# A two-layer trunk (RG-LRU, then forgetting attention): projections one step on, one tile for all pairs' keys and queries, squares behind the tanhs, sums kept in SBUF

## The chip, the cores and the metric

The kernel runs on one core of one Trainium2 chip. Its time is the device time of one execution in microseconds (us); the figure compared is the median over the runs of a kernel. TensorE is PE in the profile (its weight loads are PEld), VectorE is DVE, ScalarE is ACT, GpSimd is POOL, and SP is the engine that issues most of the DMAs and all the DMA transposes.

## The reference

The input is 1024 positions of width 1024 in float32. Two residual layers and a last norm are computed:

```python
h = rms_norm(x, g0)                       # layer 0: RG-LRU
u = h @ w_in                              # two halves of width 1536
xc = causal conv of width 4 over the first half
r, i = sigmoid(block_diag(xc, wa) + ba), sigmoid(block_diag(xc, wx) + bx)   # 12 blocks of 128
a = exp(-8 * r * softplus(-a_param))
hs = scan over positions of  a * previous + sqrt(1 - a*a) * (i * xc)
x = x + (hs * silu(second half)) @ w_out
h = rms_norm(x, g1)                       # layer 1: attention with a forget gate
q, k, v, gate, f = h @ w_in               # 16 heads of 64, f: one logit for each head
cum = cumsum(log_sigmoid(f + b_f))
p = softmax(q k^T / 8 + cum[query] - cum[key], causal)
x = x + ((p v) * silu(gate)) @ w_out
out = rms_norm(x, final_g)
```

## The kernel before

Products in full precision are made from three matmuls: both operands are cut into a high and a low part (names with `h` and `l`: `wh` and `wl` of a weight, `hh` and `hl` of the normed input, `qkh` and `qkl` of keys and queries). ACT makes the high part of a weight (line 90), DVE or POOL the low part (line 101). All matmuls are issued by the helper on line 60, most DMAs by `fetch` and the like on line 57.

**Layer 0** (up to about 430 us) loops over 12 blocks `n` of 128 channels: projections (`ups`, `gps`), convolution, two gates (tanhs on ACT, line 322), scan, and pieces of the output projection as filling work. Beside it the kernel computes the squared norm of each value weight, which later bounds the values: `squares_of_values` loads a piece of `wv` (128x512, 256 KB) into one of the `wf` buffers that the weights also use, and ACT squares and sums it (line 405). There are 16 pieces, two for each block from n = 3 on.

**Layer 1.** A prologue (430 to 560 us) makes the first values, the forget gate and pair 0's keys and queries. Heads come in pairs: head `hd` is half `s = hd % 2` of pair `hd // 2`. A projection of one half of the positions (a unit) is 24 matmuls in four steps of six. Its result goes to the tiles `qkh` and `qkl` (one set for keys, one for queries), and from there DMAs on SP's queue copy rows into the operand tiles: `T0` or `T1` for keys (one for each `s`), and for queries `U` (positions 0 to 511, shared by both `s`) and `U0` or `U1` (positions 512 to 1023).

For each head there are two stretches of work, called runs, written by a table of characters: `.` takes one step of filling work (`fill`) and one of the DMAs that load operands (`side`), a digit takes a step of attention.

- First run: `weigh(hd, 0)` (the product with the values, PSUM tile `O`) and `maxima(hd, 1)` (the logits `S` of the second 512 queries, their maximum on DVE, exp on ACT, weights `pp`, and a DMA transpose `pT<-pp` on SP's queue, line 806).
- Second run: `weigh(hd, 1)` and `maxima(hd + 1, 0)`.

The operand DMAs (`pieces`) stand on the same SP queue between the transposes. In the first run come `U` of hd + 1 and the second half of `T` of hd + 1; in the second run `U0`/`U1` of hd + 1, which `maxima(hd + 1, 1)` reads in the next run, and the first half of `T` of hd + 2. The filling of an even head is the next pair's keys (first half), queries (first half) and keys (second half); that of an odd head its queries (second half) and the gate, two halves. The key and query tiles are taken anew for each pair, in the same memory.

From head 12 on the filling is the output projection. `partial` (16 groups of 36 matmuls) loads 512 positions of the residual (`xp<-x1d`, into one of two `R` buffers), adds the product of six pairs on DVE (line 915) and stores the sum through POOL's queue (line 916). `turned` then loads the sums again (`x<-x1d`), transposes them on PE into a PSUM bank of tag `g`, adds the last two pairs' product, squares on ACT and multiplies by `grow`, the last norm's factors (line 974); only then is the bank free. `grow` is loaded behind head 15's first run into a `sg` buffer.

A scheduler with a time model of its own fixes the order of the instructions on each engine; engines and the SP queue take them strictly in that order. The pools that matter here: PSUM tags `g`, `S` and `O` with two buffers each, `wf` three, `p` two, `pp` four, `R` two.

Of the kernel before, what the change touches and what calls it, by code (L numbers as in the profile page):

```python
# [35 lines left out]
def f32(ap):  # L36
    return ap.bitcast(F32)
# [3 lines left out]
def trunk(ctx: ExitStack, tc: tile.TileContext, xt, w0, wg, wo0, pc, gn, gf, w1, wv, wf, bf, wo1, out):  # L41
# [146 lines left out]
    with ExitStack() as l0:  # L188
# [207 lines left out]

        vsq = const.tile([P, 4, 4], F32, name="vsq")

        def squares_of_values():

            for g, i in itertools.product(range(4), range(4)):
                wt = loaded((2, 256))
                nc.sync.dma_start(wt, wv[g, :, 2 * i : 2 * i + 2])
                flat = wt.rearrange("p a b -> p (a b)")
                nc.scalar.activation(flat, flat, AF.Square, accum_out=vsq[:, g, i : i + 1])
                yield
# [3 lines left out]
        for n in range(NB):  # L410
            wu = first[0] if n == 0 else list(weights(w0[n]))
            if n == 1:
                ups = both = [ps.tile([P, HALF], F32, tag="g", name="ups") for h in range(2)]
            else:
                ups = two_banks("ups")
                both = [ups.rearrange("p a b -> p (a b)")]
                ups = [ups[:, h] for h in range(2)]
            product(ups[0], 0, wu)
            if n == 0:
                gps = held[0] = two_banks("gps")  # L420
                product(gps[:, 0], 0, first[1])
# [62 lines left out]
        def value_bounds():  # L484

            g2 = const.tile([P, KT], F32, name="g2")
            nc.vector.tensor_tensor(g2, gnt[:, 1], gnt[:, 1], ALU.mult)
            g2 = g2.rearrange("p (k two) -> p k two", two=2)
            most = const.tile([P, 4], F32, name="most")
            nc.vector.tensor_tensor(most, g2[:, :, 0], g2[:, :, 1], ALU.max)  # L490
            nc.vector.tensor_tensor(vsq, vsq, most.unsqueeze(1).to_broadcast([P, 4, 4]), ALU.mult)
            all_ = ps.tile([P, 16], F32, tag="O", name="vnorm")
            matmul(all_, onesf, vsq.rearrange("p a b -> p (a b)"), start=True, stop=True)
            nc.vector.tensor_reduce(
                scale_v, all_.rearrange("p (a b) -> p a b", b=4), mybir.AxisListType.X, ALU.add
            )
# [45 lines left out]
    with ExitStack() as l1:  # L542
# [83 lines left out]
        def kq_units(pair, parts=((1, (0, 1)), (0, (0, 1)))):  # L626

            for is_k, hs in parts:
                if hs[0] == 0:
                    kq[pair, is_k] = tuple(  # L630
                        kqpool.tile([P, SEQ], F32R, tag=f"qk{p}{is_k}", name=f"qk{p}") for p in "hl"
                    )
                if hs[0] == 0 or pair == 0:
                    kqw[is_k] = list(weights(w1[is_k * 8 + pair], lo_eng=low(pair)))
                hi, lo = kq[pair, is_k]

# [12 lines left out]
        def load(hd, cs=slice(0, SEQ), us=(0, 1)):  # L649

            pair, s = hd // 2, hd % 2
            rows = slice(s * HD, (s + 1) * HD)
            hi, lo = (f32(z[rows, cs]) for z in kq[pair, 1])
            fetch(f32(T[s][:64, 0, cs]), hi)
# [7 lines left out]

        def piece(to, src):
            with tc.issue_after(turns[-3].ins):
                fetch(to, src)

        def pieces(hd, is_k, c):

# [3 lines left out]
            rows, cs = slice(s * HD, (s + 1) * HD), halves[c]  # L672
            hi, lo = (f32(z[rows, cs]) for z in kq[pair, is_k])
            if is_k:
# [5 lines left out]
            for to, from_ in todo:  # L680
                piece(f32(to), from_)
                if to is not todo[2][0]:
                    yield

        def load_q(hd, c):
            s = hd % 2
            u = U[s][c]
            hi, lo = (f32(z[s * HD : (s + 1) * HD, halves[c]]) for z in kq[hd // 2, 0])
            fetch(f32(u[:64, 0]), hi)
# [210 lines left out]
        def first_out():  # L900
            split_out(0)
            yield from ()

        def partial(todo):

            for db, c in todo:
# [3 lines left out]

                x = rpool.tile([P, HALF], F32, tag="R", name="xp")
# [3 lines left out]
                nc.vector.tensor_tensor(x, x, pt, ALU.add)  # L915
                nc.gpsimd.dma_start(x1d[c, :, db], x)

# [247 lines left out]
```

## Time and profile before

| what | value |
|---|---|
| three runs | 1108.07, 1110.34, 1109.8 us; median 1109.8 |
| profiled execution | 1107.29 us, its span 1105.5 us |
| PE busy | 1057.9 us of the span (96%) |
| DVE, ACT, POOL busy | 777.4, 613.3, 100.3 us |
| DMA | 143.08 MB in 218332 packets, 129 GB/s in the mean |

Three kinds of view are used. The stretches give, for a part of the span, the busy time of PE, PEld, DVE, ACT and POOL (with the count of instructions), the TensorE clock that was granted (1.00 is full), the busy share of the 16 DMA engines and their rate. The waits give, for an engine, what its idle time ended with: the waiting instruction's output tile and line, then engine and output of what released it, the us in total, how many times, and the longest. The order in time gives start and length in us of each instruction, and in brackets the idle time ahead of it with its releaser.

### The profile page before, as it was taken

To read this page: it belongs to the slowest core of one execution; us is meant where nothing else is said; L and a number is where in the kernel's file an instruction comes from. 1 tells how busy PE (TensorE), PEld (TensorE's weight loads), DVE (VectorE), ACT (ScalarE), POOL (GpSimd) and SP (SyncE) were. 2 spreads that over 40 slices of the span, in tenths; PEclk is the share of its full clock that TensorE was granted. 3 is DMA by queue.
4 is the path that set the end of the run, shared out by engine and by line. 5 is a ranking of instruction groups with operands and counts; after the bars stand their busy time and mean duration, and the time that the engine had idled before them with its cause. 6 is when DMAs were issued, how large, how long until landed. Compare 5 with 4: busy or idle time off the path is not lost. (4 is left out here: it accounts for less than half of the span.)

```text
span 1105.5 us, 14905 instructions
## 1 busy us (share of the span) xinstructions
PE 1057.9 (96%) x5100; PEld 849.1 (77%) x5100; DVE 777.4 (70%) x1439; ACT 613.3 (55%) x1044; POOL 100.3 (9%) x77
## 2 busy tenths in 40 slices
PE   9999999999999999999989999999998999899877
PEld 7786888888888887897767887778876797677656
DVE  7888657666677588957777758776687847756545
ACT  8498343555455464646656546564565635544425
POOL 1312021212221110210000000000000000000000
PEclk9999999999999999999999999999999999999999
DMA  6212212222121113526788838888588846899775
GB/s 240 68 53 59 60 54 66 62 67 64 61 63 52 49 29 105 166 58 168 142 179 180 182 84 177 187 159 183 113 174 194 175 121 139 221 207 224 213 188 191
DMA packets 218332, 143.08 MB, mean 129 GB/s; under 512 B 161616, under 2 KB 176464, under 8 KB 218256
## 3 DMA queue, kind: packets, MB, share of 16 engines
q1 hardware_dynamic: 216976, 137.93, 51.7%
q0 software_dynamic: 1280, 4.20, 1.2%
q8 instruction: 40, 0.66, 0.3%
q14 instruction: 36, 0.29, 0.1%
HBM read 63.30 MB, written 15.86 MB: 72 GB/s over the span
## 5 line engine op out<-in xcount | busy, mean ns | idle before, releaser
L60 PE MATMUL gps<-hh,wh 128*128 128x512 f32 x576 | 228.5, 397 | 2.7 <-DVE qkl L101 2.7
L60 PE MATMUL gps<-hh,wl 128*128 128x512 f32 x576 | 226.8, 394 | 0.7 <-DVE wl L101 0.7
L60 PE MATMUL gps<-hl,wh 128*128 128x512 f32 x576 | 226.9, 394 | 0.0
L90 ACT CAST wh<-wf 128x512 fp32r<-128x512 f32 (+2 forms) x156 | 93.8, 605 | 113.2 <-PE ops L60 47.1
L795 ACT ACTIVATE p<-S,m 128x128 f32<-128x128 f32 (+7 forms) x128 | 94.6, 740 | 87.6 <-DVE m L790 41.7
L60 PEld LDWEIGHTS gps<-hh,wh 128*128 128x128 f32 x576 | 108.8, 189 | 25.8 <-DVE qkl L101 4.4
L60 PEld LDWEIGHTS gps<-hl,wh 128*128 128x128 f32 x576 | 108.5, 188 | 25.1 <-issue 0.5
L60 PEld LDWEIGHTS gps<-hh,wl 128*128 128x128 f32 x576 | 108.8, 189 | 22.4 <-DVE wl L101 1.0
L101 POOL TENSOR_TENSOR wl<-wf,wh 128x512 fp32r<-128x512 f32 (+1 forms) x50 | 86.6, 1740 | 379.1 <-ACT wh L90 272.8
L60 PE MATMUL S<-T,U 96*128 96x512 f32 (+7 forms) x384 | 96.4, 357 | 20.2 <-DMA U<-cumd 10.4
L790 DVE CUSTOM_DVE_ANT_0 S<-S,mask 128x128 f32<-128x128 f32 (+7 forms) x128 | 97.1, 760 | 18.8 <-PE S L60 18.1
L804 DVE SCALAR_TENSOR_TENSOR pp<-p,sums,pp 128x128 f16<-128x128 f32 (+7 forms) x128 | 103.3, 813 | 9.0 <-ACT pp L92 8.3
L92 ACT ACTIVATE pp<-p,sums 128x128 f16<-128x128 f32 (+7 forms) x128 | 96.6, 770 | 20.5 <-DVE sums L802 8.2
L60 PEld LDWEIGHTS S<-T,U 128*128 128x128 f32 (+1 forms) x384 | 69.6, 192 | 38.7 <-ACT p L795 11.0
L389 DVE TENSOR_TENSOR x<-x,ops 128x512 f32<-128x512 f32 x80 | 54.1, 682 | 43.9 <-PE ops L60 43.8
L101 DVE TENSOR_TENSOR wl<-wf,wh 128x512 fp32r<-128x512 f32 x106 | 70.2, 666 | 19.0 <-ACT wh L90 18.7
L60 PE MATMUL O<-pT,v 128*128 128x512 f16 (+3 forms) x396 | 71.3, 322 | 8.7 <-DMA pT<-pp 8.6
L60 PE MATMUL ups<-hh,wh 128*128 128x512 f32 x192 | 77.1, 402 | 2.2 <-ACT wh L90 1.7
L60 PE MATMUL ups<-hh,wl 128*128 128x512 f32 x192 | 77.2, 402 | 0.9 <-POOL wl L101 0.9
L60 PE MATMUL ups<-hl,wh 128*128 128x512 f32 x192 | 77.5, 403 | 0.1
L60 PE MATMUL ops<-yh,wh 128*128 128x512 f32 x192 | 75.9, 396 | 0.5 <-DVE x L517 0.5
L60 PE MATMUL ops<-yh,wl 128*128 128x512 f32 x192 | 75.7, 394 | 0.1
(186 smaller groups left out, 1977.6 us busy)
## 6 DMA issues: line engine op xcount, KB each, us to landing
wf<-in_w SPq DMA_DIRECT2D x100, 256.0 KB
wf<-in_wo SPq DMA_DIRECT2D x64, 128.0 KB
wf<-in_wv SPq DMA_DIRECT2D x32, 256.0 KB
T<-qkh SPq DMA_DIRECT2D x64, 128.0 KB
U<-qkh SPq DMA_DIRECT2D x64, 128.0 KB
x<-in_xt SPq DMA_DIRECT2D x16, 256.0 KB
x1d<-x SPq DMA_DIRECT2D x16, 256.0 KB
T<-qkl SPq DMA_DIRECT2D x32, 128.0 KB
```

Source lines behind the costliest of these rows:

```text
L60: pe[0] = nc.tensor.matmul(*args, **kw)
L90: nc.scalar.copy(hi, src)
L92: nc.scalar.activation(hi, src, AF.Copy, scale=scale)
L101: return eng.tensor_tensor(lo, src, f32(hi), ALU.subtract)
L389: nc.vector.tensor_tensor(x, x, pt, ALU.add)
L790: nc.vector.tensor_tensor_reduce(S[:, :n], S[:, :n], mask[:, SEQ - n :], -1.0, -NEG, ALU.add, ALU.min, accum_out=m)
L795: seen[0] = nc.scalar.activation(p, S[:, :n], AF.Exp, bias=m, scale=-1.0, accum_out=sums[:, i : i + 1])
L804: nc.vector.scalar_tensor_tensor(both[:, :, 1], p, r, both[:, :, 0], ALU.mult, ALU.subtract)
```

## The change

1. **Projections one step on.** The first half of a pair's keys moves from the even head to the odd head before. Heads 2p now fill with the second half of the keys and both halves of the queries, heads 2p + 1 with the gate and the first half of the keys of pair p + 2. Head 0 has one unit more (keys of pair 1, first half), head 12 one less. The key weights of pairs 3, 5 and 7 are loaded and split a second time between the two units.
2. **Operands a run sooner.** The first run of `hd` loads both query halves of hd + 1, the second run both key halves of hd + 2. The first two DMAs of a key half go out in one step.
3. **One tile for all pairs.** `kq` holds one pair of tiles for keys and one for queries for the whole layer; units write their halves again.
4. **Squares behind tanhs.** The squares are made from 32 pieces of 128x256 (128 KB) in a buffer of their own (`wvf`, one buffer), four for each block from n = 4 on, and ordered behind the last tanh of the block before. `value_bounds` makes two small DVE multiplications in place of three operations, and `vnorm` grows from 16 to 32 columns.
5. **Sums kept in SBUF.** The sums of the first 512 positions for column blocks 3 to 7 stay in SBUF (`homes`: 3 in a `sg` buffer, 4 to 7 in the `T0` tile); their five stores through POOL go away. Blocks 0 to 2 are loaded again as three DMAs of 256 KB (into `U0` and the `sg` buffer's other half) instead of all eight blocks as eight of 128 KB and, for the second quarter, four of 256 KB. `grow` moves from a `sg` to a `p` buffer.

```diff
@@ squares_of_values, and its place in the loop over blocks
-            for g, i in itertools.product(range(4), range(4)):
-                wt = loaded((2, 256))
-                nc.sync.dma_start(wt, wv[g, :, 2 * i : 2 * i + 2])
-                flat = wt.rearrange("p a b -> p (a b)")
-                nc.scalar.activation(flat, flat, AF.Square, accum_out=vsq[:, g, i : i + 1])
+            for g, k in itertools.product(range(4), range(KT)):
+                wt = tmp.tile([P, 256], F32, tag="wvf", name="wvf")
+                nc.sync.dma_start(wt, wv[g, :, k])
+                nc.scalar.activation(wt, wt, AF.Square, accum_out=vsq[:, g, k : k + 1])
                 yield
...
-            if n > 2:
-                take(vsquares, 2)
+            if n > 3:
+                with tc.issue_after(state[n - 1]["last"].ins):
+                    take(vsquares, 4)
@@ kq_units
-                if hs[0] == 0:
-                    kq[pair, is_k] = tuple(
+                if is_k not in kq:
+                    kq[is_k] = tuple(
                         kqpool.tile([P, SEQ], F32R, tag=f"qk{p}{is_k}", name=f"qk{p}") for p in "hl"
                     )
-                if hs[0] == 0 or pair == 0:
+                if hs[0] == 0 or pair == 0 or is_k and pair in (3, 5, 7):
                     kqw[is_k] = list(weights(w1[is_k * 8 + pair], lo_eng=low(pair)))
@@ pieces
-                piece(f32(to), from_)
-                if to is not todo[2][0]:
+                piece(f32(to), from_, lag)
+                if to is not todo[2][0] and (to is not todo[0][0] or not is_k):
                     yield
@@ partial, residual
+                kept = c == 0 and db > 2
+                x = home(db) if kept else rpool.tile([P, HALF], F32, tag="R", name="xp")
                 fetch(x, x1d[c, :, db])
...
-                nc.gpsimd.dma_start(x1d[c, :, db], x)
+                if not kept:
+                    nc.gpsimd.dma_start(x1d[c, :, db], x)
...
             if c == q == 0:
-                xs = tu.tile([P, KT, 256], F32, tag="T0", name="x1")
-                xs = [xs[:, d] for d in range(KT)]
-                for d, x in enumerate(xs):
-                    fetch(x, x1d[c, :, d, cs])
-                return xs
+                two = tu.tile([P, 2, HALF], F32, tag="U0", name="x0")
+                homes[0], homes[1] = two[:, 0], two[:, 1]
+                for d in range(3):
+                    fetch(homes[d], x1d[c, :, d])
+            if c == 0:
+                return [homes[d][:, cs] for d in range(KT)]
@@ the loop over heads
-                    fill = kq_units(pair + 1, ((1, (0,)), (0, (0,)), (1, (1,))))
+                    fill = kq_units(pair + 1, ((1, (1,)), (0, (0, 1))))
+                    if hd == 0:
+                        fill = chain(kq_units(1, ((1, (0,)),)), fill)
...
-                        kq_units(7),
+                        kq_units(7, ((1, (1,)), (0, (0, 1)))),
...
-                fill = chain(kq_units(pair + 1, ((0, (1,)),)), g_units(pair + 1))
+                fill = chain(g_units(pair + 1), kq_units(pair + 2, ((1, (0,)),)))
...
-            side = chain(pieces(hd + 1, 0, 0), pieces(hd + 1, 1, 1)) if hd else iter(())
+            side = chain(pieces(hd + 1, 0, 0), pieces(hd + 1, 0, 1)) if hd else iter(())
...
-            side = pieces(hd + 2, 1, 0)
-            if hd:
-                side = chain(pieces(hd + 1, 0, 1), side)
+            side = chain(pieces(hd + 2, 1, 0), pieces(hd + 2, 1, 1))
...
-        grow = at.tile([P, SEQ], F32, tag="sg", name="grow")
+        grow = at.tile([P, SEQ], F32, tag="p", name="grow", bufs=2)
```

How the change moves the instructions is shown at three places, in the order in which an engine takes them. The first is SP's queue in the attention layer before the change, in a second run: the transposes of `maxima(hd + 1, 0)` (their shapes 128x2x128 to 128x8x128 are its four rows of queries), and between them the four DMAs of `U1`, which the next run's logits read.

```order
L806 DMA_TRANSPOSE pT_4974<-pp_4982 128x2x128
L57 DMA U1_3635<-qkh_4401 64x512
L806 DMA_TRANSPOSE pT_4974<-pp_5002 128x4x128
L57 DMA U1_3635<-qkh_4401 64x512
L806 DMA_TRANSPOSE pT_4974<-pp_5022 128x6x128
L57 DMA U1_3635<-qkl_4402 64x512
L57 DMA U1_3635<-cumd_3624 2x512
L806 DMA_TRANSPOSE pT_4974<-pp_5047 128x8x128
L57 DMA T0_3631<-qkh_4839 64x512 x2
```

The same queue after the change, in a first run (the transposes 128x10x128 to 128x16x128 belong to `maxima(hd, 1)`):

```order
L802 DMA_TRANSPOSE pT_4908<-pp_4918 128x10x128
L57 DMA U_3678<-qkl_3724 64x512
L57 DMA U_3678<-cumd_3669 2x512
L57 DMA wf_5309<-in_wv 128x512
L802 DMA_TRANSPOSE pT_4908<-pp_4941 128x12x128
L57 DMA U1_3680<-qkh_3723 64x512
L802 DMA_TRANSPOSE pT_4908<-pp_4963 128x14x128
L57 DMA U1_3680<-qkh_3723 64x512
L57 DMA U1_3680<-qkl_3724 64x512
L57 DMA U1_3680<-cumd_3669 2x512
L57 DMA T0_3676<-qkh_3681 64x512
L802 DMA_TRANSPOSE pT_4908<-pp_4986 128x16x128
```

`U1` now follows `U` in the run ahead, four transposes earlier than it stood.

The second place is ACT in layer 0 before the change, at the second pair of squares (line 405): they stand between the exps of the recurrence (lines 348, 349) and the tanhs of a gate (line 322).

```order
L322 ACTIVATE th_747<-gate_754,hba_110 128x512
L347 ACTIVATE m2_926<-th_747,c2_105 128x1024
L348 ACTIVATE a_925<-th_747,nc2_106 128x1024
L405 ACTIVATE wf_1118,vsq_236<-wf_1118 128x512
L349 ACTIVATE th_747<-a_925 128x1024
L322 ACTIVATE ti_748<-gate_759,hbx_111 128x512
L90 CAST xch_805<-xc_799 128x1024
L405 ACTIVATE wf_1121,vsq_236<-wf_1121 128x512
L322 ACTIVATE ti_748<-gate_764,hbx_111 128x512
L90 CAST yh_769<-a_700 128x1024
```

ACT after the change, at the first squares (now line 404), with the casts of the gate's weights (`wh_1126`, `wh_1132`) among them:

```order
L349 ACTIVATE th_1005<-a_1189 128x1024
L322 ACTIVATE ti_1006<-gate_1017,hbx_111 128x512
L90 CAST wh_1076<-wf_1073 128x512
L322 ACTIVATE ti_1006<-gate_1022,hbx_111 128x512
L90 CAST yh_1027<-a_919 128x1024
L404 ACTIVATE wvf_1112,vsq_236<-wvf_1112 128x256
L404 ACTIVATE wvf_1115,vsq_236<-wvf_1115 128x256
L90 CAST wh_1126<-wf_1124 128x512
L404 ACTIVATE wvf_1118,vsq_236<-wvf_1118 128x256
L404 ACTIVATE wvf_1121,vsq_236<-wvf_1121 128x256
L90 CAST wh_1132<-wf_1130 128x512
```

The squares have left the tanhs and stand in one group ahead of two weight casts.

The third place is SP's queue at the end. Before, `grow` (line 1086) was loaded ahead of the transposes of head 14's second half of queries:

```order
L57 DMA T1_3632<-qkh_8340 64x512
L57 DMA wf_9248<-in_wo1 128x512
L57 DMA xp_9154<-x1d_94 128x512
L57 DMA wf_9254<-in_wo1 128x256
L1086 DMA grow_9626<-in_gf 128x1024
L57 DMA wf_9336<-in_wo1 128x256 x2
L806 DMA_TRANSPOSE pT_9095<-pp_9105 128x10x128
```

After, it is loaded (line 1097) behind the last transpose of head 15, the last head:

```order
L57 DMA x1_9867<-x1d_94 128x2x256
L802 DMA_TRANSPOSE pT_9561<-pp_9571 128x10x128
L802 DMA_TRANSPOSE pT_9561<-pp_9598 128x12x128
L57 DMA x1_9860<-x1d_94 128x2x256
L57 DMA x1_9868<-x1d_94 128x2x256
L802 DMA_TRANSPOSE pT_9561<-pp_9629 128x14x128
L802 DMA_TRANSPOSE pT_9561<-pp_9650 128x16x128
L1097 DMA grow_9709<-in_gf 128x1024
```

So `grow` has moved past both of the last heads' transposes; the sums of the second 512 positions (`x1`) now stand ahead of it.

More of the change, by code (lines that the diff above doesn't have):

```diff
@@ L393, in two_banks @@
             return ps.tile([P, 2, HALF], F32, tag="S", name=name)
-        vsq = const.tile([P, 4, 4], F32, name="vsq")
+        vsq = const.tile([P, 4, KT], F32, name="vsq")
         def squares_of_values():
-            for g, i in itertools.product(range(4), range(4)):
-                wt = loaded((2, 256))
-                nc.sync.dma_start(wt, wv[g, :, 2 * i : 2 * i + 2])
-                flat = wt.rearrange("p a b -> p (a b)")
-                nc.scalar.activation(flat, flat, AF.Square, accum_out=vsq[:, g, i : i + 1])
+            for g, k in itertools.product(range(4), range(KT)):
+                wt = tmp.tile([P, 256], F32, tag="wvf", name="wvf")
+                nc.sync.dma_start(wt, wv[g, :, k])
+                nc.scalar.activation(wt, wt, AF.Square, accum_out=vsq[:, g, k : k + 1])
                 yield
@@ L484, in value_bounds @@
         def value_bounds():
[L486 to L492, printed above, removed]
+            for _ in range(2):
+                nc.vector.tensor_tensor(vsq, vsq, gnt[:, 1].unsqueeze(1).to_broadcast([P, 4, KT]), ALU.mult)
+            all_ = ps.tile([P, 4 * KT], F32, tag="O", name="vnorm")
             matmul(all_, onesf, vsq.rearrange("p a b -> p (a b)"), start=True, stop=True)
             nc.vector.tensor_reduce(
-                scale_v, all_.rearrange("p (a b) -> p a b", b=4), mybir.AxisListType.X, ALU.add
+                scale_v, all_.rearrange("p (a b) -> p a b", b=KT), mybir.AxisListType.X, ALU.add
             )
@@ L628, in kq_units @@
             for is_k, hs in parts:
-                if hs[0] == 0:
-                    kq[pair, is_k] = tuple(
+                if is_k not in kq:
+                    kq[is_k] = tuple(
                         kqpool.tile([P, SEQ], F32R, tag=f"qk{p}{is_k}", name=f"qk{p}") for p in "hl"
                     )
-                if hs[0] == 0 or pair == 0:
+                if hs[0] == 0 or pair == 0 or is_k and pair in (3, 5, 7):
                     kqw[is_k] = list(weights(w1[is_k * 8 + pair], lo_eng=low(pair)))
-                hi, lo = kq[pair, is_k]
+                hi, lo = kq[is_k]
                 def use(h, pt):
@@ L652, in load @@
             rows = slice(s * HD, (s + 1) * HD)
-            hi, lo = (f32(z[rows, cs]) for z in kq[pair, 1])
+            hi, lo = (f32(z[rows, cs]) for z in kq[1])
             fetch(f32(T[s][:64, 0, cs]), hi)
@@ L661, in trunk, with piece, pieces @@
         turns = []
-        def piece(to, src):
-            with tc.issue_after(turns[-3].ins):
+        def piece(to, src, lag):
+            with tc.issue_after(turns[-lag].ins):
                 fetch(to, src)
-        def pieces(hd, is_k, c):
+        def pieces(hd, is_k, c, lag=3):
             if hd >= HEADS:
@@ L672, in pieces @@
             rows, cs = slice(s * HD, (s + 1) * HD), halves[c]
-            hi, lo = (f32(z[rows, cs]) for z in kq[pair, is_k])
+            hi, lo = (f32(z[rows, cs]) for z in kq[is_k])
             if is_k:
@@ L687, in load_q @@
             u = U[s][c]
-            hi, lo = (f32(z[s * HD : (s + 1) * HD, halves[c]]) for z in kq[hd // 2, 0])
+            hi, lo = (f32(z[s * HD : (s + 1) * HD, halves[c]]) for z in kq[0])
             fetch(f32(u[:64, 0]), hi)
@@ L902, in first_out, with home @@
             yield from ()
+        homes = {}
+        def home(db):
+            if db == 3:
+                two = at.tile([P, 2, HALF], F32, tag="sg", name="x3")
+                homes[3], homes[2] = two[:, 0], two[:, 1]
+            elif db == 4:
+                four = tu.tile([P, 4, HALF], F32, tag="T0", name="x4")
+                homes.update((4 + i, four[:, i]) for i in range(4))
+            return homes[db]
         def partial(todo):
@@ L909, in partial @@
                     split_out(db + 1)
-                x = rpool.tile([P, HALF], F32, tag="R", name="xp")
+                kept = c == 0 and db > 2
+                x = home(db) if kept else rpool.tile([P, HALF], F32, tag="R", name="xp")
                 fetch(x, x1d[c, :, db])
```

## The prediction

> **What bounds the kernel now.** I read the page's head first, then the stretches, then what PE waited for, and last the order in time around those waits.
>
> ```profile
> span 1105.5 us, 14905 instructions
> ...
> PE 1057.9 (96%) x5100; PEld 849.1 (77%) x5100; DVE 777.4 (70%) x1439; ACT 613.3 (55%) x1044; POOL 100.3 (9%) x77
> ```
>
> PE is the bound: it idles 1105.5 - 1057.9 = 47.6 us. Whatever the change gains is idle PE time, or time in which the granted clock is low. The stretches show where those lie (length; busy time of PE, PEld, DVE, ACT, POOL; clock; DMA share; GB/s):
>
> ```profile
> 0.00:125.00 125.00, 120.67 (x495) 95.14 (x496) 99.71 (x121) 87.61 (x120) 24.24 (x21) 0.99 0.30 98
> 125.00:430.00 305.00, 305.00 (x1321) 247.94 (x1320) 214.47 (x230) 156.45 (x200) 57.12 (x31) 1.00 0.20 59
> ...
> 560.00:940.00 380.00, 363.51 (x1956) 293.75 (x1955) 265.84 (x654) 213.20 (x425) 0.00 (x0) 1.00 0.75 160
> 940.00:1047.00 107.00, 95.68 (x421) 71.64 (x419) 66.79 (x152) 51.05 (x98) 6.67 (x12) 0.97 0.90 218
> 1047.00:1100.00 53.00, 46.67 (x248) 36.51 (x248) 28.59 (x58) 23.18 (x56) 2.17 (x4) 0.97 0.69 196
> ```
>
> From 125 to 430 PE never idles. The heads in steady state (560 to 940) lose 16.5 us in gaps, the end (940 to 1100) 11.3 + 6.3 = 17.6 us, and by its clock of 0.97 about 160 x 0.03 = 5 us more. The waits of PE over the span name the gaps (us, times, longest):
>
> ```profile
> PE S L60 <- DMA U<-cumd: 10.4, 8, 2.0
> PE O L60 <- DMA pT<-pp: 8.6, 5, 3.3
> PE S L60 <- ACT p L795: 7.5, 6, 2.4
> PE gps L60 <- DVE qkl L101: 2.7, 4, 1.2
> PE turn L60 <- DVE xp L915: 2.4, 1, 2.4
> PE ups L60 <- ACT wh L90: 1.7, 1, 1.7
> PE S L60 <- ACT yo L833: 1.6, 2, 0.8
> ...
> PE ups L60 <- POOL wl L101: 0.9, 1, 0.9
> PE turn L60 <- DMA x<-x1d: 0.8, 1, 0.8
> ...
> PE S L60 <- DMA U<-qkh: 0.6, 1, 0.6
> ```
>
> Some gaps cost twice, since the clock falls behind them. Around two of them:
>
> ```profile
> 104.00:108.00 4.00, 3.01 (x8) 2.16 (x9) 4.00 (x3) 3.97 (x7) 3.90 (x2) 0.72 0.18 49
> 108.00:112.00 4.00, 4.00 (x17) 3.19 (x16) 3.64 (x5) 3.93 (x5) 1.19 (x1) 0.85 0.25 84
> 704.00:708.00 4.00, 2.66 (x10) 2.26 (x11) 1.77 (x5) 0.89 (x2) 0.00 (x0) 0.82 0.85 174
> 708.00:712.00 4.00, 4.00 (x17) 3.32 (x16) 1.40 (x6) 1.51 (x3) 0.00 (x0) 0.76 0.88 254
> ```
>
> The lost clock is 4 x (0.28 + 0.15) = 1.7 us at the first and 4 x (0.18 + 0.24) = 1.7 us at the second place. The same price fits the end: 5 us there are three such falls.
>
> **The steady heads.** Moving `U0`/`U1` from the second run to the first puts one whole run between its DMAs and the logits that read it; today the last of its four DMAs ends the wait. All waits on `U` are 10.4 + 0.6 = 11.0 us, with 1.7 us of clock 12.7. What could be late next is ACT and DVE, busy 213.2 and 265.8 of 380 us (56 and 70%); of the waits on them S<-p is 7.5 us, mostly at the end. Each run still issues eight operand DMAs between four transposes on SP's queue, so nothing is added to that queue. Bounds: -12.7, and -5 if the freed time runs into that chain. I take -11.5, near the first.
>
> The single key and query tiles let a unit write half of a tile while DMAs still read the other half; before, a new tile waited for every reader of the old one (gps<-qkl, 2.7 us, with S<-yo 1.6 us beside it). The first half of the keys is now written at the end of an odd head, some dots behind the DMAs that read that half, so a new wait there could be as long as the old one. Bounds: -4.3 and 0; I take -2.
>
> The moved unit (24 matmuls, 5.5 us) goes from head 12 to head 0 and changes no sum. The key weights read again cost six loads of 256 KB, six casts and six subtractions:
>
> ```profile
> L90 ACT CAST wh<-wf 128x512 fp32r<-128x512 f32 x144 | 88.1, 616 | 99.0 <-PE ops L60 47.1 <-PE gps L60 23.2 <-issue 15.7
> ...
> L101 DVE TENSOR_TENSOR wl<-wf,wh 128x512 fp32r<-128x512 f32 x98 | 66.8, 686 | 13.7 <-ACT wh L90 13.4
> ```
>
> That is 6 x (0.62 + 0.69) = 7.9 us on engines that idle 30 to 44% of the stretch. The step's DMAs stand on SP ahead of the unit, as those of the queries do today, on which no PE wait shows. Bounds: 0, and +7.9 without that cover; I take 0.
>
> **Layer 0.** The two waits of 1.7 and 0.9 us at 104 to 106 follow two squares on ACT, which hold up the tanhs of a gate and with them the weight cast:
>
> ```profile
> 94.93 0.63 ACT L405 ACTIVATE wf<-wf 128x512 f32<-128x512 f32 x1 [0.76 <-DMA wf<-in_wv]
> 98.91 0.63 ACT L405 ACTIVATE wf<-wf 128x512 f32<-128x512 f32 x1 [0.78 <-DMA wf<-in_wv]
> ...
> 104.08 0.50 PE L60 MATMUL ups<-hh,wh 128*128 128x512 f32 x1 [1.68 <-ACT wh L90]
> 105.96 0.80 PE L60 MATMUL ups<-hh,wl 128*128 128x512 f32 x1 [0.92 <-POOL wl L101]
> ```
>
> They cost 2 x 0.63 + 1.54 = 2.8 us on ACT, as much as the gaps; without them there the gaps and the 1.7 us of clock go, 4.3 us. Later blocks pay for it: four loads through one buffer, each issued only when the square before is done.
>
> ```profile
> ACT wf L405 <- DMA wf<-in_wv: 40.0, 15, 5.0
> ...
> 207.69 0.63 ACT L405 ACTIVATE wf<-wf 128x512 f32<-128x512 f32 x1 [4.75 <-DMA wf<-in_wv]
> 211.62 0.63 ACT L405 ACTIVATE wf<-wf 128x512 f32<-128x512 f32 x1 [3.21 <-DMA wf<-in_wv]
> ...
> DMA to landing us min/median/max: 2.3/4.2/7.7
> ```
>
> (The last row is of the `xp` loads of 256 KB, in the crowded end.) ACT idles (305 - 156.5) / 12 = 12.4 us in a block of 25.4 us, and 4.75 + 3.21 = 8 us of waiting in one block left no gap on PE. Three chained loads wait 6.9 us at 2.3 us each, 12.6 us at 4.2. DMA is busy only 20% there, so I stand near the first: hidden. Bounds: -4.3 and +4; I take -3.5.
>
> The Trainium skill (DMA: Bandwidth & Descriptors, "Rules for kernel authors") advises coalescing small transfers, and its fit in the section on the anatomy of a DMA gives about 2.0 us and bytes over 436 GB/s: by estimate 16 x 2.6 = 42 us for the old loads, 32 x 2.3 = 74 us for the new. The old waits of 40.0 us agree with it; it speaks against this part, and by it a block would wait 6.9 us, still under the 12.4.
>
> **The end.** The two waits of `turn` on an `xp` sum and a reloaded `x` (2.4 + 0.8 = 3.2 us) go, since column blocks 4 to 7 of the first half need no store and no load. Five stores of 256 KB and 1.25 MB of loads less are 11.5 us of transfer at the 218 GB/s of that stretch; the waits O<-pT and S<-p there may shrink. From 940 on they are
>
> ```profile
> PE O L60 <- DMA pT<-pp: 7.5, 3, 3.3
> PE S L60 <- ACT p L795: 5.1, 4, 2.4
> ```
>
> of which 2.5 us of O<-pT come behind the last logits (below) and stay. Bounds: 0 and -8.4 (the other 5.0 and two falls of the clock); I take -3, nearer zero, since S<-p and the transposes follow the chain of ACT and DVE.
>
> Against it stands `grow`, now behind the last transpose.
>
> ```profile
> 1047.11 1.20 PE L60 MATMUL S<-T,U 128*128 128x512 f32 x4 [0.28 <-ACT p L795]
> ...
> 1053.35 2.35 DVE L804 SCALAR_TENSOR_TENSOR pp<-p,sums,pp 128x896 f16<-128x896 f32 x2 [0.58 <-ACT pp L92]
> ...
> 1057.02 7.29 SPq L806 DMA_TRANSPOSE pT<-pp  x2
> ...
> 1057.53 0.60 PE L60 MATMUL O<-pT,v 128*128 128x256 f16 x4 [2.51 <-DMA pT<-pp]
> ```
>
> Count from the last logits (1047.11). The last `pp` is ready 8.6 us later; the last transpose is through between 11 us (two at 1.2 us without a queue) and 17.2 us (as today). `grow` lands 2.3 to 7.7 us after that, 14 + 4.2 = 18.2 in the middle, and one multiplication of 0.7 us frees the first bank: 18.9. By the new order PE has 18 `ops` matmuls, the products O and the first two parts of `turned` ahead of the third part; with the wait for pT (10.4, as today) it is there at about 13.7. The third part needs that bank, since `g` has two: a stall of 5.2 us, with 1.7 us of clock 6.9. Bounds: 0.3, and 11.9 + 1.7 = 13.6. The load of `x3` waits for `gated(13, 1)`, which holds a bank too: 0 to 1.8 us, I take 0.9 (nothing shows it).
>
> The end sums to -3.2 - 3 + 6.9 + 0.9 = +1.6.
>
> **Sum.** -11.5 - 2 + 0 - 3.5 + 1.6 = -15.4 on the profiled 1107.3 us: 1091.9. The median of the runs lies 2.5 us above that execution, so I forecast 1094.4 us. All low bounds together give 1107.3 - 12.7 - 4.3 - 4.3 - 11.3 + 2.5 = 1077.2, all high ones 1107.3 - 5 + 0 + 7.9 + 4 + 12.2 + 2.5 = 1128.9 (the end by itself is -3.2 - 8.4 + 0.3 = -11.3 or -3.2 + 13.6 + 1.8 = +12.2).
>
> The Trainium skill (TensorE: Matmul & The Clock Gate, "HAM oscillation — how this bites in real kernels") has the clock halve behind idle gaps above 3.4 us. By it the gaps here are too short, the two 1.7 us at closed gaps would not come back, and the sum would be 3.4 us higher, 1097.8; the trace disagrees, with 0.72 and 0.85 behind gaps of 1.7 and 0.9 us.
>
> **Rivals.**
> - Forecast, 1094 (own range 1088 to 1100): 0.53.
> - The end gains as well: `grow` early enough (0.3 in place of 6.9) and the O<-pT waits gone (-8.4 in place of -3), 12 us less: 1082. The 90% DMA share speaks for it, the ACT and DVE chain against. 0.12.
> - PE, freed of `U`, meets the chain of maxima, exps and weights: half the gain (-6) and nothing from the tiles: 1102. DVE's 70% speaks against, the 7.5 us of S<-p for. 0.16.
> - Slower: the chained squares. If a load waits 5.0 us, the longest now, three make 15 us against 12.4 us of idle ACT, 2.6 us on PE in each of eight blocks, 21 us, with no gain of 4.3 at 104; behind such gaps the clock may fall too (8 x 1.7). That gives 1094.4 + 3.5 + 21 = 1119, up to 1133. It decides from about 4.6 us a load: then (13.9 - 12.4) x 8 = 12 us eat the 11.9 that the other parts bring. For it: the casts of gate weights stand behind the squares. Against: a queue at 20%. 0.19, with cases near no change inside.
>
> About 0.2% is what a measurement here can tell from no change, 2 us: faster 0.76, same 0.05, slower 0.19. The range 1081 to 1113 leaves out about half of the slow case and a little below.
>
> **What would show it.** In 560 to 940 the row S<-U goes from 11 us to about nothing, and PE busy rises over 98%; at 104 no gap; in 125 to 430 PE stays at 305 of 305, though waits on `wvf` add up to 60 us or more; at the end a wait of `turn` on `res` appears, 5 us, behind `grow`. I am wrong if gaps on `wh` appear every block, if S<-p takes over the 11 us, or if `grow` is late by 10 us and more.

## The result and the profile after

The changed kernel takes 1092.33 us (median; 1091.87 to 1096.85), the kernel before 1108.93 in the runs beside it; the ratio is 0.9867, with a 95% interval of 0.9826 to 0.9908, some 14.7 us less. The forecast was 1094.4 us in a range of 1081 to 1113. The sum came out, but two of its terms were far off in opposite directions, as the stretches and the experiments below show. One of the twelve executions of e11 took 2698.56 us and is not counted in any figure here.

The head of the page of the changed kernel, then its stretches (columns as in the prediction):

```profile
span 1090.1 us, 15016 instructions
...
PE 1051.2 (96%) x5100; PEld 845.4 (78%) x5100; DVE 782.7 (72%) x1444; ACT 619.2 (57%) x1082; POOL 100.8 (9%) x72
```

```profile
0.00:125.00 125.00, 123.04 (x517) 97.78 (x518) 101.39 (x123) 88.81 (x123) 28.49 (x22) 1.00 0.30 96
125.00:430.00 305.00, 305.00 (x1321) 247.94 (x1320) 218.48 (x236) 161.89 (x237) 55.90 (x31) 1.00 0.20 61
...
560.00:940.00 380.00, 366.58 (x1979) 296.19 (x1978) 274.38 (x670) 219.49 (x437) 0.00 (x0) 1.00 0.79 167
```

The first row has 2.4 us more PE work than before: the gaps at 104 us are gone. The second is full, as before. The third is the surprise: the heads idle 380 - 366.6 = 13.4 us, against 16.5 before; the prediction had them nearly free of waits. PE is idle 38.9 us of the span (47.6 before), 8.7 us less; the other 6.7 us of the 15.4 by which the span is shorter are PE busy time, mostly matmuls that no longer run at half clock.

What PE waited for, over the span of the changed kernel:

```profile
PE S L60 <- DMA U<-cumd: 7.2, 7, 2.6
PE S L60 <- ACT p L791: 6.8, 8, 1.6
PE ops L60 <- DVE xp L924: 2.7, 1, 2.7
PE ops L60 <- DVE x L924: 2.6, 1, 2.6
PE O L60 <- DMA pT<-pp: 2.4, 3, 1.4
PE turn L60 <- DVE res L985: 2.3, 1, 2.3
PE turn L60 <- ACT yhh L90: 2.2, 1, 2.2
PE vps L60 <- ACT wh L90: 1.3, 1, 1.3
```

S<-U is still the largest, 7.2 us; gps<-qkl and S<-yo are gone; O<-pT is 2.4 instead of 8.6. The waits on U are other ones than before. SP's queue in order of time, at the longest:

```profile
708.52 2.23 SPq L57 DMA_DIRECT2D U<-qkh  x2
710.80 0.58 SPq L57 DMA_DIRECT2D wf<-in_w  x1
711.43 0.91 SPq L57 DMA_DIRECT2D wf<-in_wv  x2
712.45 1.39 SPq L802 DMA_TRANSPOSE pT<-pp  x1
713.89 0.75 SPq L57 DMA_DIRECT2D U<-qkl  x1
714.70 0.44 SPq L57 DMA_DIRECT2D U<-cumd  x1
```

and PE there:

```profile
718.83 0.36 PE L60 MATMUL S<-T,U 96*128 96x256 f32 x1 [2.63 <-DMA U<-cumd]
```

The shape 96x256 belongs to the first 512 queries. Before, the waits had 96x320, the second 512; one of them, and SP's queue behind it:

```profile
705.34 0.69 PE L60 MATMUL S<-T,U 96*128 96x320 f32 x3 [1.68 <-DMA U<-cumd]
```

```profile
713.93 1.40 SPq L806 DMA_TRANSPOSE pT<-pp  x1
715.38 0.63 SPq L57 DMA_DIRECT2D U<-qkl  x1
716.06 0.45 SPq L57 DMA_DIRECT2D U<-cumd  x1
```

After the change the last two DMAs of `U` stand behind three weight loads and a transpose, are issued at 714, and land too late. `U` stood behind that transpose before the change too; then PE came later, held up by `U1` in the run ahead. With that wait closed, `U` was next.

ACT became late as well. Among the waits of 560 to 940 us, where S<-p had no row before, stands now

```profile
PE S L60 <- ACT p L791: 3.5, 5, 0.8
```

At the end, `grow` is as late as forecast. SP's, DVE's and PE's rows (the last logits begin at 1036.5):

```profile
1042.61 6.07 SPq L802 DMA_TRANSPOSE pT<-pp  x2
1048.74 0.57 SPq L1097 DMA_DIRECT2D grow<-in_gf  x1
```

```profile
1053.59 1.29 DVE L985 TENSOR_TENSOR res<-turn,grow 128x512 f32<-128x512 f32 x2 [6.21 <-DMA grow<-in_gf]
```

```profile
1046.71 0.51 PE L60 MATMUL turn<-woh,yhh 128*128 128x512 f32 x1 [2.20 <-ACT yhh L90]
...
1054.34 0.66 PE L60 MATMUL turn<-ident,x 128*128 128x128 f32 x4 [2.28 <-DVE res L985]
```

DVE gets `grow` 17.1 us after the last logits (the prediction had 18.2). PE is at the third part after 15.5 us, not 13.7, so the stall is 2.28 us and not 5.2. The wait ahead of it is on `yhh`, where the prediction had one on pT, and it ends about as forecast (after 10.2 us; 10.4 forecast). But the matmuls behind it run at a clock of 0.54 and 0.60 (1048 to 1050 and 1050 to 1052 us), and PE needs 5.3 us from there to the third part, in place of 3.3. Each of the two waits brings a fall of the clock.

### The profile page after: what moved, and what is told of

Read it like the earlier page. It is cut to its first block, busy times and chain, and to the rows that moved or that the text cites. A ratio compares the mean times of both kernels' runs of the same rounds, so it can differ in the third digit from the quotient of the medians.

```text
span 1090.1 us, 15016 instructions
## 1 busy us (share of the span) xinstructions
PE 1051.2 (96%) x5100; PEld 845.4 (78%) x5100; DVE 782.7 (72%) x1444; ACT 619.2 (57%) x1082; POOL 100.8 (9%) x72
## 3 DMA queue, kind: packets, MB, share of 16 engines
q1 hardware_dynamic: 218336, 138.19, 52.7%
## 5 line engine op out<-in xcount | busy, mean ns | idle before, releaser
L90 ACT CAST wh<-wf 128x512 fp32r<-128x512 f32 (+2 forms) x162 | 97.4, 605 | 130.7 <-PE ops L60 43.7
L101 POOL TENSOR_TENSOR wl<-wf,wh 128x512 fp32r<-128x512 f32 (+1 forms) x50 | 89.8, 1805 | 372.5 <-ACT wh L90 368.7
L800 DVE SCALAR_TENSOR_TENSOR pp<-p,sums,pp 128x128 f16<-128x128 f32 (+7 forms) x128 | 103.3, 814 | 11.5 <-ACT pp L92 10.3
L101 DVE TENSOR_TENSOR wl<-wf,wh 128x512 fp32r<-128x512 f32 x112 | 74.3, 667 | 31.7 <-ACT wh L90 31.5
L60 PE MATMUL vps<-wh,hh 128*128 128x256 f32 (+1 forms) x256 | 73.4, 287 | 1.6 <-ACT wh L90 1.3
```

Source lines behind the costliest of these rows:

```text
L60: pe[0] = nc.tensor.matmul(*args, **kw)
L90: nc.scalar.copy(hi, src)
L101: return eng.tensor_tensor(lo, src, f32(hi), ALU.subtract)
L800: nc.vector.scalar_tensor_tensor(both[:, :, 1], p, r, both[:, :, 0], ALU.mult, ALU.subtract)
```

## The experiments

Each is compared with the kernel before on the same chip; 0.001 of the ratio is 1.1 us. The medians come from several chips, on which the kernel before takes 1104.8 to 1108.9 us, so two runs compare best by their ratios.

| run | ratio | 95% interval | median, us |
|---|---|---|---|
| changed kernel | 0.9867 | 0.9826 to 0.9908 | 1092.33 |
| e1 squares alone | 0.9997 | 0.9981 to 1.0014 | 1107.97 |
| e2 move alone (parts 1 to 3) | 0.9863 | 0.9837 to 0.9890 | 1091.84 |
| e3 sums alone | 0.9922 | 0.9902 to 0.9943 | 1098.33 |
| e4 changed, grow early | 0.9796 | 0.9773 to 0.9818 | 1085.41 |
| e5 one tile alone | 0.9983 | 0.9961 to 1.0006 | 1104.27 |
| e7 changed, old squares | 0.9908 | 0.9882 to 0.9934 | 1095.34 |
| e8 e4 with U early | 0.9910 | 0.9884 to 0.9936 | 1095.62 |
| e9 changed, no kept sums | 0.9845 | 0.9816 to 0.9874 | 1088.45 |
| e10 as e8, head 3 left | 0.9846 | 0.9819 to 0.9873 | 1090.79 |
| e11 e1 and a delay on PE | 1.0043 | 1.0023 to 1.0064 | 1112.18 |
| e12 e2, unit back in head 12 | 0.9971 | 0.9949 to 0.9994 | 1103.74 |
| e13 e3, grow early | 0.9922 | 0.9891 to 0.9953 | 1098.11 |

### Each part alone

e1 has only the changes of `squares_of_values`, its call and `value_bounds`:

```diff
-            if n > 2:
-                take(vsquares, 2)
+            if n > 3:
+                with tc.issue_after(state[n - 1]["last"].ins):
+                    take(vsquares, 4)
```

> The kernel before with part 4 alone (squares behind the tanhs, 32 pieces of 128x256). The prediction's term was -3.5 us, with bounds -4.3 and +4; the trace of the changed kernel has no gap of PE between 8 and 431 us, which reads as the whole -4.3 (2.6 us of gaps at 104 and 106 us and 1.7 us of clock). If that reading is right: 4 us less than before, no wait of ups on wh or wl at 104, PE busy 305 of 305 from 125 to 430, clock 1.00 there. Rival (the chained loads cost PE something that the other parts hide in the changed kernel): a time within 1 us of before, and waits on wh behind line 404.

Measured: nothing, 0.9997. The gaps at 104 us are gone and 125 to 430 is full, as the first reading had it, but the time isn't there. From the first logits on all engines take the same order as before, and yet the heads of that execution wait more for `U` (11.0 us before) and its clock falls eight times instead of five. Waits and a stretch of e1:

```profile
PE S L60 <- DMA U<-cumd: 11.1, 9, 2.0
...
PE S L60 <- DMA U<-qkh: 4.0, 4, 1.3
```

```profile
566.00:570.00 4.00, 0.84 (x4) 0.68 (x5) 1.62 (x3) 0.61 (x1) 0.00 (x0) 1.00 0.80 160
570.00:574.00 4.00, 4.00 (x14) 3.26 (x13) 1.17 (x4) 0.88 (x2) 0.00 (x0) 0.57 0.93 225
```

e2 has parts 1 to 3:

> The kernel before with parts 1 to 3 alone (projections one step on, operands a run sooner, one tile). By the prediction's terms -11.5 - 2 = -13.5 us. By the trace of the changed kernel less: its heads still wait 7.2 us for U (now for the first 512 queries, at the start of a second run), 3.5 us for S<-p where there was none, and 1.3 us for value weights, so idle time from 560 to 940 fell only from 16.5 to 13.4 us; with one fall of the clock (1.7 us) and the 4.3 us of qkl and yo already counted in, about -5 us. So -13.5 against -5; S<-U about 7 us by the second, near 0 by the first.

Measured: 0.9863, about 15.2 us, more than either number. S<-U is 6.1 us, as the second reading had it, so the rest came from elsewhere. From 940 us on e2 waits:

```profile
PE ops L60 <- DVE xp L915: 4.2, 2, 2.9
PE turn L60 <- ACT yhh L90: 3.5, 1, 3.5
PE O L60 <- DMA pT<-pp: 1.5, 2, 1.0
...
PE S L60 <- ACT p L795: 0.5, 1, 0.5
```

O<-pT and S<-p were 7.5 and 5.1 us before. At the end e2 changes only two things: the unit that left head 12, and the place of the last heads' operand loads.

e3 has part 5:

> The kernel before with part 5 alone (sums of the first 512 positions kept in SBUF, grow in a p buffer). The prediction's end sums to +1.6 us. The traces of before and after, from 940 us on, show idle time falling from 17.6 to 14.0 us and one to two falls of the clock fewer (1.7 us each): about -5 us. Rival: that gain of the end comes from the unit that has left head 12, not from the sums; then this kernel is 0 to 2 us slower than before, with a wait of turn on res behind grow of 2 us or more.

Measured: 0.9922, 8.6 us less, more than the 5 of the first reading; the rival falls, and so does the prediction's +1.6 for this part on the kernel before. O<-pT over the span is 2.2 us there. The parts don't add up: e2 and e3 together have 24 us, the changed kernel 14.7. Both remove the same waits on pT at the end (O<-pT from 940 us on: 7.5 us before, 1.5 in e2, 1.3 in e3, 1.4 in the changed kernel).

e5 has part 3 alone (`kq[is_k]` in place of `kq[pair, is_k]`, with the tiles made once):

> The kernel before with part 3 alone: one tile for all pairs' keys and queries, so that a unit may write one half while the other is read; units and operand DMAs stay where they were. If the wait of a new tile for all readers of the old one is what holds gps<-qkl, that wait (2.7 us) goes and S<-U stays at 10 to 15 us: 2 to 3 us less than before. Rival: gps<-qkl comes from reads of the same half, then it stays and the time is that of before within 2 us.

Measured: 0.9983, 1.9 us with an interval that touches 0. No row gps<-qkl is left among its waits, as the first reading said, but S<-U grew from 11.0 us to

```profile
PE S L60 <- DMA U<-cumd: 14.5, 10, 3.1
```

PE comes sooner to operands that come no sooner. That limits what a gain ahead of `U` can bring on this kernel, though a part of a shift does reach the end, as e11 shows below.

### The parts taken out of the changed kernel

e7 is the changed kernel with the old squares:

> The changed kernel with part 4 undone (squares as before: 16 pieces of 128x512 among the tanhs). Alone on the kernel before, part 4 closed the gaps at 104 us and yet gave nothing measurable (0.9997), although all engines take the same order behind layer 0; the waits on U there were 4.1 us longer and the clock fell more often. If a gain of layer 0 is always lost to later waits, this kernel takes the time of the changed one within 2 us (1090 to 1094). If it was lost only because U was the wait next in line, which the move of the operands shortens, this kernel is 3 to 5 us slower than the changed one: 1095 to 1097.

Measured: 0.9908 against 0.9867, 4.5 us slower, the second reading, though the intervals overlap. e9 is the changed kernel without kept sums:

> The changed kernel with part 5 undone (all sums stored and loaded again, grow in its sg buffer, loaded early); behind layer 0 every engine takes the order of the run with the move alone (1091.8 us). If part 5 as it stands gives and takes about the same (its gain of some 7 us against grow's late load, 6.9 us), this kernel takes the time of the changed one, 1090 to 1094. If the squares' 4.3 us reach the end here: 1087 to 1089. If the sums bring in the changed kernel what they bring alone (8.5 us): 1098 to 1101.

Measured: 0.9845, between the first two readings by the ratio, with the median in the second: part 5 as it stands costs the changed kernel about 2 us (0.9867 - 0.9845; the intervals overlap), where alone it brings 8.6.

### grow

e4 is the changed kernel with `grow` in other memory, ahead of the last four transposes in SP's queue; PE, ACT and DVE take exactly the same order:

```diff
-        grow = at.tile([P, SEQ], F32, tag="p", name="grow", bufs=2)
+        grow = tu.tile([P, SEQ], F32, tag="U", name="grow")
...
-                res = [tu.tile([P, SEQ], F32, tag=t, name="res") for t in ("U", "U0")]
+                res = [at.tile([P, SEQ], F32, tag="p", name="res", bufs=2), tu.tile([P, SEQ], F32, tag="U0", name="res")]
```

> The changed kernel with grow in the memory of U, which is free after head 15's first half of logits, so that its load is issued ahead of the last four transposes (one result tile takes the p buffer in its place). In the changed kernel turn waits 2.28 us on res at 1054 us, behind grow, and the clock falls after it. If grow is what costs: the wait goes, 2.3 to 4 us less than the changed kernel, that is about 1088 to 1090 us. Rival: the first multiplication is late because of DVE's queue or because PE waits elsewhere first (turn on yhh, 2.2 us, stands just ahead of it); then the wait stays or moves to pT, and the time is that of the changed kernel within 1 us.

Measured: 0.9796, 1085.41 us, 6.9 us less than the changed kernel by the medians, more than the 2.3 to 4 of the first reading. The wait of `turn` on `res` is gone. The two profiles differ by 6.4 us: e4 is 2.3 us ahead at the last wait on a sum already (996.4 against 998.7), which has nothing to do with `grow`; the other 4.1 are the stall of 2.28 and one fall of the clock. This is the fastest kernel of the study.

e13 gives the same to e3 (same two lines):

> The kernel before with part 5 alone, and grow in the memory of U, loaded ahead of the last transposes (the one result tile in the p buffer). Part 5 alone took 0.9922 with grow late (turn<-res 2.0 us and no wait of turn on xp or x). If grow costs there what it cost in the changed kernel (6.9 us): 1090 to 1093. If only its own wait of 2.0 us goes: 1095 to 1097. Together with the run of the changed kernel with early grow (0.9796) it shows how much of the move's 15 us is left beside the sums: 7 us by the first reading, 11 by the second.

Measured: 0.9922, as without it. The first reading is ruled out; the second isn't, since the interval covers 1095 to 1097 us. The wait `turn<-res` (2.0 us in e3) goes here too. From 940 us on e13 waits

```profile
PE S L60 <- ACT p L795: 7.6, 3, 3.3
```

as e3 does (7.3 us). The last of these waits ends at 1041.7, at the last logits, and the clock falls behind it, which it doesn't at that place in e3: from the last logits to the end of the span e3 takes 52.7 us and e13 52.1. So in these two executions a fall of the clock took back what the closed wait gave. In e4, with the move, S<-p has no row from 940 us on. Beside early `grow` and sums, the move still brings 0.9922 - 0.9796, 14 us (the squares are in that difference too).

### The unit that left head 12

e12 is e2 with the unit computed a second time in head 12:

```diff
-                        kq_units(7, ((1, (1,)), (0, (0, 1)))),
+                        kq_units(7, ((1, (0,)), (1, (1,)), (0, (0, 1)))),
```

> The run with the move alone (1091.8 us, 0.9863 of before), with the unit put back into head 12 that had left it: the first half of pair 7's keys is projected a second time there (24 matmuls, 5.5 us, the same values written again), so PE's work is 5.5 us more than before. In the run with the move alone the waits O<-pT and S<-p from 940 us on fell from 7.5 and 5.1 to 1.5 and 0.5 us, which the prediction had not put to the move. If the operand loads (a run sooner, out of the way of the transposes) did that, the waits stay small and the time is 5 to 6 us more: 1097 to 1098. If the missing unit did it (the output projection comes a unit sooner to the waits), they come back, 5 to 11 us on top: 1102 to 1108. If the extra unit fills waits: under 1095.

Measured: 1103.74, 11.9 us more than e2 (by the two intervals, some 4 us either way), of which the 24 matmuls are 5.5. The unit also loads and splits pair 7's key weights once more (two loads of 256 KB); no wait of PE for them shows. From 940 us on the waits came back:

```profile
PE O L60 <- DMA pT<-pp: 6.3, 3, 3.0
PE S L60 <- ACT p L795: 3.0, 3, 1.7
PE turn L60 <- DVE xp L915: 2.6, 1, 2.6
```

O<-pT is back at 6.3 of 7.5 us, S<-p at 3.0 of 5.1, and the idle time of PE from 940 us on, 23.2 us before and 16.7 in e2, is 22.2. So most of what the move removed at the end hangs on the missing unit, and not on the operand loads, which e12 has where e2 has them. Without the unit the output projection comes a unit sooner against the last heads; that this is how the waits go is the likely reading, and no run separates it from the weights that the unit loads.

### The operands of U, and a delay

e8 puts the last two DMAs of `U` ahead of the transpose, on top of e4:

```diff
-            side = chain(pieces(hd + 1, 0, 0), pieces(hd + 1, 0, 1)) if hd else iter(())
+            side = chain(pieces(hd + 1, 0, 0, 5), pieces(hd + 1, 0, 1)) if hd else iter(())
```

> The changed kernel with grow in the memory of U, as in the run before, and with the first four operand DMAs of a first run tied to the fifth transpose back instead of the third, so that the last two of U's DMAs stand ahead of the transpose 128x10x128 and of the value weights' loads. In the changed kernel and in the run with grow alone the heads still wait 7.2 and 5.8 us for U<-cumd, the longest (1.4 to 2.6 us) where value weights are loaded in between. If that place in the queue is the cause: S<-U near 0, 4 to 6 us less than the 1085.4 us of the run with grow alone, that is 1080 to 1082. Rival: the operands are late because of the queue's transfers, not its order; then S<-U stays at 5 us or S<-p takes the time over, and the kernel takes 1084 to 1087.

Measured: 1095.62, 10 us slower than e4. No wait on `U` is left: its place in the queue was the cause. In its stead stands one wait for weights, since the scheduler moved other loads as well (PE, then SP's queue):

```profile
629.67 0.79 PE L60 MATMUL gps<-hh,wh 128*128 128x512 f32 x1 [14.13 <-ACT wh L90]
```

```profile
624.65 1.22 SPq L802 DMA_TRANSPOSE pT<-pp  x1
625.91 1.05 SPq L57 DMA_DIRECT2D wf<-in_w  x2
```

A pair of weight loads slipped behind the transposes of a whole run. e10 leaves head 3 as it was (`5 if hd != 3 else 3`):

> As the run with early operands (grow in the memory of U, first four operand DMAs of a first run tied to the fifth transpose back), but head 3 left as in the changed kernel. In that run S<-U was gone, as expected, and 14.1 us of waiting for one pair of weights came in its place at 616 us: in head 3 the loads of a key weight had slipped behind the next run's transposes. If that was the whole loss: S<-U at 1 us (head 3's own), no wait on wh over 2 us, 4 to 6 us less than the run with grow alone, 1079 to 1081. If weights slip elsewhere too, or S<-p takes over: 1084 and more.

Measured: 1090.79, still slower than e4. Head 3's own `U` is late by 2.4 us, and a weight is late at nearly the same place as in e8:

```profile
613.22 0.36 PE L60 MATMUL S<-T,U 96*128 96x256 f32 x1 [2.37 <-DMA U<-cumd]
631.30 0.79 PE L60 MATMUL gps<-hh,wh 128*128 128x512 f32 x1 [5.01 <-ACT wh L90]
```

Neither run could show what earlier operands are worth while the weights keep their place; that stays open.

e11 is e1 with 48 small matmuls of ones on PE between the layers:

> The kernel before with part 4 alone (0.9997 of before), and 48 small matmuls of ones put on PE between the two layers (at 0.09 us each, 4.3 us; their result isn't used). They put back about the time that part 4 gains in layer 0. If that gain is swallowed by the attention layer because its heads are paced by something that starts no sooner or by waits that grow as PE comes earlier, the delay is swallowed as well: 1106 to 1109, as without it. If the gain reaches the end and was lost by chance of the clock in those runs: 4 us more, 1110 to 1113.

Measured: 1112.18, 4.2 us more than e1 by the medians, 5.1 by the ratios, in the range of the second reading. But the delay was 2.5 times as long as planned, since the 48 calls show as 96 matmuls of 0.11 us each:

```profile
431.02 10.88 PE L60 MATMUL warm<-onesf 128*128 128x128 f32 x96
```

PE begins the first logits of the attention layer at 505.7 us in e1, 510.7 before and 516.8 in e11; the spans end at 1104.5, 1105.5 and 1110.1. So of the 11.1 us between e1 and e11 5.6 are left at the end, and of the 5.0 us by which e1 was ahead of the kernel before, 1.0. The attention layer takes up a good part of a shift, with the same order on every engine, and the time fits the second reading only because the delay was too long. Much of that part is clock: the lost clock (span times one minus the mean clock), averaged over runs, is 14.0 us in e1, 10.3 in e11 and 12.8 in the kernel before (beside e1), of which 1.7 lay in the gap that e1 closed. Behind layer 0 e1 so loses 2.9 us more than the kernel before. The rest, and why the clock falls more often where PE comes sooner, stays open.

## Why the prediction was right, and where it was not

**The total** was 2 us off. By terms:

- **Layer 0, -3.5.** The gaps closed, -4.3 on the spot. What reached the end was 0 alone (e1), about -2 beside the move (e9 against e2) and about -4.5 in the changed kernel (e7), with intervals that overlap each time. The chained loads stayed hidden, as argued: ACT waits for them

```profile
ACT wvf L404 <- DMA wvf<-in_wv: 45.4, 24, 2.8
```

  24 times, three for each of eight blocks, 1.9 us each and 5.7 us a block; the prediction had 6.9, and 60 us or more in all. (The fit that it quotes from the Trainium skill, DMA: Bandwidth & Descriptors, "Anatomy of one DMA", is given there for DMAs that GpSimd issues; these are issued by SP.) Its limit of 12.4 us was miscounted: it divided 305 us by twelve blocks, but the first squares of the eight blocks stand at 113.6 to 376.0 us, 37.5 us apart, in which ACT idles some 18 us. So the slow rival needed not 4.6 but over 6 us a load; its 0.19 rested on too low a limit.
- **Steady heads, -11.5 - 2: this step failed.** Idle time from 560 to 940 fell by 3.1 us in the changed kernel (4.9 in e2: 11.6 us left), with one fall of the clock 4.8 (6.6) us. The mechanism was right for `U1` and the tiles; the step "what could be late next is ACT and DVE" was right for the smaller part only, the 3.5 us of S<-p. First came `U`, 7.2 us, on the same queue, whose DMAs the prediction had counted as "nothing added" without asking when PE would now want them. e8 showed it by moving them. So two of the prediction's own signs failed: S<-U is not "about nothing", and PE is busy 96.5% of 560 to 940 us, not over 98%.
- **The moved unit, 0: this step failed.** "Changes no sum" was right for PE's work and wrong for the waits: e12 puts 11.9 - 5.5 = 6.4 us on its place, some 4 us either way. The prediction looked at head 12's filling only as time.
- **The end, +1.6.** Measured about +2 (changed kernel against e9; the intervals overlap), and its parts agree in size: `grow` +6.9 forecast, 6.9 by the medians (e4), the rest -5.3 forecast, -5.4 measured (e4 against e9, 0.0049). Both agreements are luck in part. `grow` is a stall of 2.28, not 5.2, a fall of the clock, and 2.3 us that the profile doesn't put to `grow`. Of the rest, the waits of `turn` on `xp` and `x` (3.2) are gone without kept sums already (no such row in e2 and e9). The gain of 3 on O<-pT and S<-p was laid to fewer transfers; most of these waits go with the unit (O<-pT from 940 us on is 1.5 us in e2 and 3.8 in e9), and the sums alone remove O<-pT only (e3: 1.3, with S<-p at 7.3). Some 2.5 us between e9 and e4 are clock (6.5 and 4.1 us lost).

So -13.5 for the move was near -15.2, with 4.8 to 6.6 us from the place named and 6.4 from one that was priced at 0. The total was right because two errors cancel, which is luck.

## What to carry to other kernels

When a wait on a queue is moved earlier, the next thing late can be the next item of the same queue, as `U` was here: check when each of its items is wanted once PE is sooner, and not only that their count stays the same. A piece of filling work moved out of the tail is worth more than its own time, or less, because it shifts the rest against the waits there; price its place by an experiment that puts it back. Loads that are needed last should still be queued ahead of transposes that wait: one 512-KB load cost 4.1 us at the end by the profiles, 6.9 by the medians, for want of a buffer that was free earlier; beside e3, where other waits and the clock set the end, moving it brought nothing measurable. And measure a delay that you put in before you read anything from it: the one of e11 was 10.9 us in place of the 4.3 meant.

## What the runs showed of the hardware

The granted clock carries a good part of these differences. Over the runs of a kernel, the lost clock is about 12 us before, 8.2 us in the changed kernel and 4.1 us in e4, so 4 us of the 14.7 are clock. How a gap becomes a fall isn't its length alone. In the changed kernel the longest wait, 2.63 us up to 718.8, leaves the clock full, and the two waits of 2.2 and 2.3 us at the end don't (the second and third row show the fall behind the first of them, the fourth the fall behind the other):

```profile
718.00:722.00 4.00, 3.17 (x15) 2.71 (x16) 1.66 (x9) 1.91 (x4) 0.00 (x0) 1.00 1.19 233
1046.00:1050.00 4.00, 3.07 (x11) 1.99 (x11) 0.70 (x2) 1.30 (x3) 0.00 (x0) 0.77 1.08 206
1050.00:1054.00 4.00, 2.06 (x8) 1.35 (x7) 0.41 (x1) 0.69 (x2) 0.00 (x0) 0.80 0.83 249
1054.00:1058.00 4.00, 3.66 (x14) 2.56 (x15) 1.47 (x4) 0.47 (x1) 0.00 (x0) 0.62 0.02 7
```

The Trainium skill (TensorE: Matmul & The Clock Gate, "What's actually happening") describes a window of 3413 ns that runs freely and isn't tied to the kernel; gaps of one length that fall or don't would fit it, while its limit of a whole idle window doesn't fit falls behind gaps of 2.2 us.
